# A hybrid decoder layer: the token-major copies of k and v are made by VectorE and DRAM instead of TensorE

## The chip, the cores and the metric

The kernel runs on one core of one Trainium2 chip. The metric is device time in microseconds (us) of one launch. Before the change it is 2226.82 us, the median of three runs (2225.97 to 2227.2).

## The reference, cut to what matters

One layer works on 16 meta tokens followed by 2048 tokens of width 1024. After an RMS norm one projection makes everything: for the gated DeltaNet 8 heads of q, k, v and a gate z (128 columns each), for the short convolution four more groups of 1024 columns. For a head the recurrence is

```python
S = S * gl + einsum('cd,ce->de', k_dec, v_new)      # once per chunk
v_new = u - einsum('cd,de->ce', w, S)
o = einsum('cd,de->ce', q_dec, S) + einsum('ij,je->ie', qk, v_new)
```

The projection produces k and v with the 128 channels on the partitions and the tokens along the free axis (channel-major). The recurrence needs k (scaled by a decay, `kd`) and v (scaled by the inverse norm of k, `vr`) with the tokens of a chunk of 128 on the partitions (token-major). The change is about how these two copies are made. The output is the layer's result with the residual added, after a last RMS norm.

## The kernel before, in words

The tokens are worked on in two halves of 1024 (`hf` 0 and 1). Each half has 8 slots, one per head; head number `i` runs from 0 to 15 over both halves. A slot is a list of projection jobs (`slot_jobs`, L825): q, k, c, h, b, the short convolution's gate, v, z. A job (`run_group`, L750) multiplies 128 columns of the input projection with all tokens of the half in three passes of split float32 (`wh*hh`, `wh*hl`, `wl*hh`), for which one 512 KB block of weights `wr` is loaded (`load_w`), rounded by ScalarE into `wh`, and subtracted by VectorE into `wl`. Both the raw block and the split are double buffered.

TensorE's instructions are put in order by hand: generators (streams) yield the time they want to wait by a planner's model of every engine (`Model`, L30), and `pump` (L234) resumes those that are due between the matmuls of the jobs. The order of TensorE, VectorE, ScalarE and GpSimd is the program order that comes out of this. The order of the DMA issues on SyncE's queue is not fixed by hand; each issue waits there for its semaphores, in order.

For each head these streams run beside the jobs of later slots:

- `delta_front` (L975): the decay matrix E, the products k·k and q·k, and a substitution of 32 steps on VectorE (`nb`, `XT`), which needs k and q of the head. Its result goes to DRAM (`xtd`).
- `normalize` (L526, first half only): the norm of a block of tokens of the second half. It uses the buffers tagged `kd`, `gw` and `Q`.
- `delta_back` (L1124): loads the blocks of the inverse (`W<-xtd`, L1135), loads `qd` (L1140), turns k, v and q with TensorE (L1148 to L1177), and merges the 32-blocks of the inverse to 128-blocks in four steps of small matmuls (`X`, `Q`, `W`, `p1` to `p4`).
- `delta_scan` (L1304): the recurrence over 8 chunks, with `kd`, `vr`, `qd`, `W`.
- `delta_out` (L1354): norm, gate and store.

`held` and `hold` (L581) keep two streams from using one buffer tag at a time: `ta` for the two PSUM banks of the streams, `Q` and `gw` for two SBUF buffers. In `delta_back` each of the six groups of four transposes (two each for k, v and q) goes through a `ta` bank: ScalarE reads k's with the scale `cd`, VectorE reads v's with the scale `ir`, ScalarE squares q's. The done mark `("vr", i)` lets the v job of the next slot overwrite `vT` (`pre_v`, L841).

After the two halves comes the output projection: 32 units of 48 matmuls (`unit_mm`, L1459).

Of the kernel before, what the change touches and what calls it, by code (L numbers as in the profile page):

```python
# [9 lines left out]
F32 = mybir.dt.float32  # L10
# [9 lines left out]
NM = 16  # L20
NH = 8
# [152 lines left out]
def hybrid_trunk(  # L174
# [23 lines left out]
    xtd = tc.dram_tile([2, 32, 32, 32], F32, name="xtd")  # L198
    ged = tc.dram_tile([2, NH * 9, 128], F32, name="ged")
    nmd = tc.dram_tile([2, NM, NM], F32, name="nmd")  # L200
    gtd = tc.dram_tile([2, NH * 9, 128], F32, name="gtd")
# [29 lines left out]
    def start(gen):  # L231
        streams.append([gen, clk()])
# [350 lines left out]
    def hold(tag="ta", keep=False):  # L583

        while tag in held:
            yield 0.2
        if keep:
            held.add(tag)

    G = {}  # L590
# [384 lines left out]
    def delta_front():  # L975

        for i in range(2 * NH):
# [144 lines left out]
            done.add(("front", i))  # L1122

    def delta_back():  # L1124

        for i in range(2 * NH):
# [18 lines left out]
            vr = vt(dp, [128, NC, 128], "vr")  # L1145
            while ("conv", hf, 16 + hd, LAST[hf]) not in done:
                yield 0.3
            for b4 in range(2):  # L1148
                cs = slice(4 * b4, 4 * b4 + 4)
                yield after(slot=(pta, "ta"), least=0.3)  # L1150
                yield from hold()
                pk = ptile(pta, "ta", [128, 4, 128])
                for c in range(4):
                    tr(pk[:, c, :], k_[:, 4 * b4 + c, :])
                for c in range(4):
                    cc = 4 * b4 + c
                    nc.scalar.activation(kd[:, cc], pk[:, c, :], AF.Copy, scale=cd[:, cc : cc + 1])
                yield after(d["vT"], slot=(pta, "ta"), least=0.3)
                yield from hold()
                pv = ptile(pta, "ta", [128, 4, 128])  # L1160
                for c in range(4):
                    c0 = m0 + 128 * (4 * b4 + c)
                    tr(pv[:, c, :], d["vT"][:, c0 : c0 + 128])
                nc.vector.tensor_tensor(
                    out=vr[:, cs],
                    in0=pv,
                    in1=ir[:, cs].unsqueeze(2).to_broadcast([128, 4, 128]),
                    op=ALU.mult,
                )
                yield after(slot=(pta, "ta"), least=0.3)  # L1170
                yield from hold()
                pq = ptile(pta, "ta", [128, 4, 128])
                for c in range(4):
                    tr(pq[:, c, :], q_[:, 4 * b4 + c, :])
                for c in range(4):
                    cc = 4 * b4 + c
                    nc.scalar.activation(junk[:, 0:128], pq[:, c, :], AF.Square, accum_out=ssq[:, cc : cc + 1])  # L1177
            done.add(("vr", i))
            egl = vt(dp, [128, NC], "egl")

            yield after(W)
            for a in (0, 64, 32):
# [14 lines left out]
            for a in (0, 64):  # L1197
                nc.scalar.activation(Q[a + 32 : a + 64, :, 0:32], p1[a + 32 : a + 64, :, 0:32], AF.Copy)
            nc.vector.tensor_copy(egl, qd[:, :, 127])
            nc.vector.tensor_tensor(out=qd, in0=qd, in1=q_, op=ALU.mult)  # L1200
# [27 lines left out]
            nc.scalar.mul(W[0:64, :, 64:128], p4[0:64], -1.0)  # L1228
            yield after(W, qd)
            blocks[i] = dict(egl=egl, kd=kd, vr=vr, P=P, qd=qd, cj=B["cj"])  # L1230
# [163 lines left out]

    LANDING = 3.0
    STEP = 1.0
    SUBST = 0.8
# [108 lines left out]
    pump()  # L1506
    start(delta_front())
    start(delta_back())
    start(delta_scan())
# [142 lines left out]
```

## Time and profile before

| | us |
|---|---|
| median of three runs | 2226.82 |
| profiled execution, its own time | 2231.35 |
| its span in the trace | 2229.6 |
| TensorE (PE) busy | 2176.5 |
| VectorE (DVE) busy | 1454.9 |
| ScalarE (ACT) busy | 851.3 |
| GpSimd (POOL) busy | 195.8 |

Busy time is the time in which at least one instruction of the engine was running; PE is the matrix multiply, PEld its weight load. "L118" stands on nearly all rows, since a helper records every instruction; so the rows are told apart by the names of their tiles: `ta<-ident,k` is a transpose of k into a `ta` bank. The share of the DMA engines is the mean over the core's 16.

### The profile page before, as it was taken

The numbers are of one execution on the slowest core, as the hardware profiler recorded it, in microseconds if no ns is written. First come the engines' busy times: TensorE is split into PE (matmuls) and PEld (weight loads), VectorE is DVE, ScalarE is ACT, GpSimd is POOL, SyncE is SP. The second block draws the span as 40 slices with busy tenths as digits, with TensorE's granted clock in tenths as the row PEclk, the third lists the DMA queues.
The fourth block names the chain that finished last, engine by engine and source line by source line (L and its number), as shares of the span: only waits on it lengthen the run. The fifth ranks groups of instructions, "written<-read, shape, count | busy, mean of one in ns | idle before, by whom it ended". The sixth has DMA issues, their size and how long they took to land.

```text
span 2229.6 us, 35449 instructions
## 1 busy us (share of the span) xinstructions
PE 2176.5 (98%) x13472; PEld 1917.2 (86%) x13472; DVE 1454.9 (65%) x3911; ACT 851.3 (38%) x1991; POOL 195.8 (9%) x361
## 2 busy tenths in 40 slices
PE   6999999999999999999999999999999999999998
PEld 5999999999999999878888888888878887788886
DVE  4677777777777777776767767676657683444222
ACT  5533434343434444443434352434342533322111
POOL 4010101010101010201010110010000100000000
PEclk9999999999999999999999999999989998999999
DMA  5434444353548844534254424353846443645321
GB/s 141 82 79 67 84 72 94 64 97 60 100 56 108 88 88 62 131 54 77 55 78 54 82 51 87 50 83 65 66 37 73 88 118 114 212 157 188 114 90 57
DMA packets 257096, 196.26 MB, mean 88 GB/s; under 512 B 61957, under 2 KB 226318, under 8 KB 256926
## 3 DMA queue, kind: packets, MB, share of 16 engines
q1 hardware_dynamic: 256926, 194.00, 46.0%
q8 instruction: 106, 1.74, 0.3%
q14 instruction: 64, 0.52, 0.1%
HBM read 157.89 MB, written 36.06 MB: 87 GB/s over the span
## 4 chain that ended last, share of the span: by engine, by line
PE 92%; DMA 2%; DVE 2%; ACT 2%; issue 1%; SPq 0%; POOLq 0%; ACTq 0%; DVEq 0%
PE mm L118 78%; PE ta L118 7%; PE rec L118 4%; PE o L118 3%; DMA wr<-in_w_in_dram 1%; ACT junk L118 1%; SPq L118 0%; DVE prod L118 0%; DVE hl L118 0%; DMA xtd<-XT 0%; DMA wr<-mixd 0%; DMA ysd<-raw 0%; DVE XT L118 0%; DVE acc L118 0%; ACT hh L118 0%
## 5 line engine op out<-in xcount | busy, mean ns | idle before, releaser
L118 PE MATMUL mm<-hh,wh 128*128 128x512 f32 (+3 forms) x2816 | 1006.3, 365 | 10.2 <-ACT hh L118 8.6
L118 PE MATMUL mm<-hl,wh 128*128 128x512 f32 (+3 forms) x2816 | 986.2, 358 | 0.2 <-DVE hl L118 0.2
L118 PE MATMUL mm<-hh,wl 128*128 128x512 f32 (+3 forms) x2816 | 641.4, 360 | 4.6 <-DVE wl L118 4.6
L118 PEld LDWEIGHTS mm<-hh,wh 128*128 128x128 f32 x2816 | 532.0, 190 | 61.5 <-ACT hh L118 9.8
L118 PEld LDWEIGHTS mm<-hl,wh 128*128 128x128 f32 x2816 | 531.9, 189 | 47.5 <-DVE hl L118 1.1
L118 PEld LDWEIGHTS mm<-hh,wl 128*128 128x128 f32 x2816 | 480.7, 189 | 53.6 <-DVE wl L118 5.5
L118 DVE TENSOR_TENSOR wl<-wr,wh 128x512 fp32r<-128x512 f32 x348 | 230.5, 685 | 69.3 <-ACT wh L118 34.1
L118 DVE SCALAR_TENSOR_TENSOR acc<-raw,pcol,acc 128x384 f32<-128x384 f32 (+2 forms) x360 | 231.3, 644 | 50.3 <-ACT acc L118 42.5
L118 ACT ACTIVATE wh<-wr 128x1024 fp32r<-128x1024 f32 x178 | 187.9, 1056 | 133.8 <-PE mm L118 88.1
L118 DVE SCALAR_TENSOR_TENSOR prod<-nb,XT 128x8 f32<-128x8 f32 (+30 forms) x496 | 194.3, 392 | 11.2 <-DMA nb<-nbd 6.4
L118 DVE TENSOR_REDUCE XT<-prod 128x8 f32<-128x16 f32 (+30 forms) x496 | 147.3, 297 | 17.1
L118 ACT ACTIVATE raw<-mm 128x384 f32<-128x384 f32 (+2 forms) x120 | 61.7, 514 | 227.8 <-PE mm L118 227.7
L118 ACT ACTIVATE vn<-rec,cj 128x128 f32<-128x128 f32 x128 | 46.9, 367 | 219.2 <-PE rec L118 218.8
L118 ACT ACTIVATE sc_c<-mm 128x384 f32<-128x384 f32 (+3 forms) x82 | 42.3, 516 | 176.1 <-PE mm L118 169.7
L118 PE MATMUL mm<-oh,wh 128*128 128x512 f32 x256 | 101.9, 398 | 0.0
L118 PE MATMUL mm<-ol,wh 128*128 128x512 f32 x256 | 100.4, 392 | 0.0
L118 DVE SCALAR_TENSOR_TENSOR yy<-rec,neg,vr 128x128 f32<-128x128 f32 x128 | 44.6, 349 | 71.6 <-PE rec L118 70.8
L118 DVE TENSOR_TENSOR y<-mm,y 128x512 f32<-128x512 f32 x23 | 15.9, 692 | 111.4 <-PE mm L118 111.4
L118 ACT ACTIVATE ojk<-y 128x512 bf16<-128x512 f32 x23 | 14.5, 631 | 183.4 <-DVE y L118 127.2
L118 POOL TENSOR_TENSOR opy<-mo,nhalf 128x4 f32<-128x4 f32 x32 | 33.7, 1052 | 509.4 <-DVE mo L118 509.4
L118 ACT ACTIVATE acc<-mm,pcol 128x384 f32<-128x384 f32 (+2 forms) x120 | 72.1, 601 | 0.1
L118 DVE SCALAR_TENSOR_TENSOR S<-S,egl,rec 128x128 f32<-128x128 f32 x104 | 35.8, 344 | 53.8 <-PE rec L118 53.5
(242 smaller groups left out, 2530.3 us busy)
## 6 DMA issues: line engine op xcount, KB each, us to landing
wr<-in_w_in_dram SPq DMA_DIRECT2D x128, 512.0 KB, 7.9
wr<-mixd SPq DMA_DIRECT2D x50, 512.0 KB, 4.5
E<-gtd SPq DMA_DIRECT2D x16, 512.0 KB, 3.8
qd<-ged SPq DMA_DIRECT2D x16, 512.0 KB, 3.9
nb<-nbd SPq DMA_DIRECT2D x64, 128.0 KB, 4.4
mixd<-zs SPq DMA_DIRECT2D x32, 256.0 KB, 2.4
out_dram<-y SPq DMA_DIRECT2D x16, 512.0 KB, 2.6
kd<-in_x_dram SPq DMA_DIRECT2D x9, 512.0 KB, 9.8
```

The source lines that it names most:

```text
L118: r = real(*args, **kw)
```

## The change

A new stream `delta_turn` runs for each head. Once all of k (and later all of v) of the head has been made, it takes each in two halves of four chunks. VectorE transposes the 32 x 32 blocks of a [128, 512] piece into a buffer (`gw` and `Q` in turn), and four DMAs of 64 KB write the buffer to a DRAM tile `kvd`, each block to its transposed place, in runs of 32 floats. `delta_back` waits for the mark `("turned", i)`, keeps only the two groups of transposes of q, and loads `kd` and `vr` token-major from `kvd` behind the load of `W`. GpSimd multiplies `kd` by its scale in the middle of the merges, VectorE multiplies `vr` at their end.

```diff
+    kvd = tc.dram_tile([2, 2, NC, 128, 128], F32, name="kvd")
...
+    def turn_out(dram, src, tmp):
+        nc.vector.transpose(out=tmp.rearrange("p c i -> p (c i)"), in_=src.rearrange("p c i -> p (c i)"))
+        for a in range(4):
+            nc.sync.dma_start(
+                dram[:, :, 32 * a : 32 * a + 32].rearrange("c (b y) x -> y (c b) x", b=4),
+                tmp[32 * a : 32 * a + 32].rearrange("y c (b x) -> y (c b) x", b=4),
+            )
...
+    def delta_turn():
+        for i in range(2 * NH):
+            hf, hd = divmod(i, NH)
+            m0 = NM if hf == 0 else 0
+            while i >= 2 and ("blocks", i - 2) not in done:
+                yield 0.3
+            for w in range(2):
+                while ("conv", hf, (8, 16)[w] + hd, LAST[hf]) not in done:
+                    yield 0.3
+                src = slot[i]["k"] if w == 0 else slot[i]["vT"][:, m0 : m0 + HALF].rearrange("p (c i) -> p c i", i=128)
+                for c2, tag in enumerate(("gw", "Q")):
+                    yield after(src, slot=(dp, tag), eng="DVE", lag=0.3)
+                    yield from hold(tag, True)
+                    cs = slice(4 * c2, 4 * c2 + 4)
+                    turn_out(kvd[i % 2, w, cs], src[:, cs], vt(dp, [128, 4, 128], tag))
+                    if w and c2:
+                        done.add(("vr", i))
+                    yield DRAIN
+                    held.discard(tag)
+            done.add(("turned", i))
...
     def delta_back():
...
-            while ("conv", hf, 16 + hd, LAST[hf]) not in done:
+            while ("turned", i) not in done:
                 yield 0.3
             for b4 in range(2):
-                cs = slice(4 * b4, 4 * b4 + 4)
-                yield after(slot=(pta, "ta"), least=0.3)
-                yield from hold()
-                pk = ptile(pta, "ta", [128, 4, 128])
-                for c in range(4):
-                    tr(pk[:, c, :], k_[:, 4 * b4 + c, :])
-                for c in range(4):
-                    cc = 4 * b4 + c
-                    nc.scalar.activation(kd[:, cc], pk[:, c, :], AF.Copy, scale=cd[:, cc : cc + 1])
-                yield after(d["vT"], slot=(pta, "ta"), least=0.3)
-                yield from hold()
-                pv = ptile(pta, "ta", [128, 4, 128])
-                for c in range(4):
-                    c0 = m0 + 128 * (4 * b4 + c)
-                    tr(pv[:, c, :], d["vT"][:, c0 : c0 + 128])
-                nc.vector.tensor_tensor(
-                    out=vr[:, cs],
-                    in0=pv,
-                    in1=ir[:, cs].unsqueeze(2).to_broadcast([128, 4, 128]),
-                    op=ALU.mult,
-                )
                 yield after(slot=(pta, "ta"), least=0.3)
                 yield from hold()
                 pq = ptile(pta, "ta", [128, 4, 128])
...
-            done.add(("vr", i))
             egl = vt(dp, [128, NC], "egl")
-            yield after(W)
+            yield after(W) + 1.5
+            for w, t_ in enumerate((kd, vr)):
+                nc.sync.dma_start(t_, kvd[i % 2, w].rearrange("c t j -> t c j"))
...
+            nc.gpsimd.tensor_tensor(
+                out=kd, in0=kd, in1=cd.unsqueeze(2).to_broadcast([128, NC, 128]), op=ALU.mult
+            )
             nc.vector.tensor_copy(egl, qd[:, :, 127])
...
             nc.scalar.mul(W[0:64, :, 64:128], p4[0:64], -1.0)
-            yield after(W, qd)
+            yield after(vr, eng="DVE", lag=0.3) + 1.0
+            nc.vector.tensor_tensor(
+                out=vr, in0=vr, in1=ir.unsqueeze(2).to_broadcast([128, NC, 128]), op=ALU.mult
+            )
+            yield after(W, qd, kd, vr)
...
+    DRAIN = 4.0
...
+    start(delta_turn())
```

## Rows read from the trace of the kernel before

**Rows 1.** The page: busy us of two engines; the chain that ended last.

```profile
PE 2176.5 (98%) x13472; PEld 1917.2 (86%) x13472; DVE 1454.9 (65%) x3911; ACT 851.3 (38%) x1991; POOL 195.8 (9%) x361
PE 92%; DMA 2%; DVE 2%; ACT 2%; issue 1%; SPq 0%; POOLq 0%; ACTq 0%; DVEq 0%
```

**Rows 2.** Windows: stretch, length, PE, PEld, DVE, ACT, POOL busy, clock, DMA share, GB/s.

```profile
64.00:1830.00 1766.00, 1750.05 (x11457) 1569.94 (x11457) 1281.78 (x3579) 723.99 (x1759) 159.84 (x271) 1.00 0.47 76
700.00:745.00 45.00, 45.00 (x289) 44.97 (x288) 38.24 (x115) 16.67 (x37) 4.42 (x10) 1.00 0.97 113
1625.00:1638.00 13.00, 13.00 (x101) 10.34 (x101) 5.30 (x10) 3.37 (x6) 0.49 (x1) 0.50 0.52 65
```

**Rows 3.** Groups by shape, TensorE: busy us, mean ns | idle before, releaser.

```profile
L118 PE MATMUL ta<-ident,vT 128*128 128x128 f32 x128 | 20.0, 279 | 1.3 <-ACT junk L118 0.7
L118 PE MATMUL ta<-ident,k 128*128 128x128 f32 x128 | 19.2, 272 | 0.7 <-DVE vr L118 0.7
```

**Rows 4.** Timeline of TensorE, head 4: start us, duration us, instruction.

```profile
633.95 0.34 PE L118 MATMUL mm<-hl,wh 128*128 128x384 f32 x1
634.12 0.60 PE L118 MATMUL ta<-ident,k 128*128 128x128 f32 x4
634.48 0.42 PE L118 MATMUL mm<-hh,wh 128*128 128x384 f32 x1
634.74 0.34 PE L118 MATMUL mm<-hl,wh 128*128 128x384 f32 x1
```

**Rows 5.** Groups by shape, VectorE.

```profile
L118 DVE TENSOR_TENSOR vr<-ta,ir 128x512 f32<-128x512 f32 x32 | 22.1, 691 | 28.1 <-PE ta L118 27.9
L118 DVE STREAM_TRANSPOSE X<-W 32x256 f32<-32x256 f32 x48 | 20.7, 432 | 11.8 <-DMA W<-xtd 10.8
L118 DVE TENSOR_TENSOR E<-E,cj 128x1024 f32<-128x1024 f32 x16 | 19.8, 1235 | 0.0
```

**Rows 6.** Queue in 636 to 641 us (W loads alone): packets, MB, share of 16 engines.

```profile
q1 hardware_dynamic: 1100, 0.13, 17.1%
```

**Rows 7.** The same in 673 to 676.4 us, mostly the four nbd writes.

```profile
q1 hardware_dynamic: 1251, 0.21, 34.8%
```

**Rows 8.** DMA issues of the whole run: count, KB each, median us to landing.

```profile
wr<-in_w_in_dram SPq DMA_DIRECT2D x128, 512.0 KB, 7.9
sc_c<-xnd SPq DMA_DIRECT2D x3, 512.0 KB, 3.6
```

**Rows 9.** Timeline of SyncE's queue, head 4: its qd load, then its xtd stores.

```profile
579.65 0.34 SPq L118 DMA_DIRECT2D qd<-ged  x1
629.85 2.13 SPq L118 DMA_DIRECT2D xtd<-XT  x4
```

**Rows 10.** Timeline: v of heads 4 and 11 complete (ScalarE), head 11's transposes (TensorE).

```profile
582.84 0.51 ACT L118 ACTIVATE vT<-acc 128x384 f32<-128x384 f32 x1
1377.17 0.63 ACT L118 ACTIVATE vT<-acc 128x512 f32<-128x512 f32 x1 [1.56 <-DVE acc L118]
1389.11 0.60 PE L118 MATMUL ta<-ident,k 128*128 128x128 f32 x4
```

**Rows 11.** Timeline: a weight rounded after a late load; idle us and releaser in brackets.

```profile
737.07 1.06 ACT L118 ACTIVATE wh<-wr 128x1024 fp32r<-128x1024 f32 x1 [0.86 <-DMA wr<-in_w_in_dram]
```

**Rows 12.** Timeline near 932 us: GpSimd, VectorE twice, TensorE.

```profile
931.73 2.81 POOL L118 TENSOR_TENSOR wl<-wr,wh 128x1024 fp32r<-128x1024 f32 x1 [1.59 <-ACT wh L118]
931.47 0.14 DVE L118 SCALAR_TENSOR_TENSOR msm<-mnb,mXT 16x5 f32<-16x5 f32 x1
932.56 2.00 DVE L118 SCALAR_TENSOR_TENSOR msm<-mnb,mXT 16x6 f32<-16x6 f32 x1
935.23 0.66 PE L118 MATMUL ta<-ident,sc_c 128*128 128x128 f32 x4 [1.85 <-DVE hl L118]
```

**Rows 13.** Timeline near 1620 us, head 13's merge: VectorE, TensorE.

```profile
1619.63 0.43 DVE L118 STREAM_TRANSPOSE X<-W 32x256 f32<-32x256 f32 x1 [7.20 <-DMA W<-xtd]
1620.16 0.22 PE L118 MATMUL ta<-X,E 32*32 32x32 f32 x2 [1.57 <-ACT junk L118]
```

## The prediction

> **What bounds the kernel now.** I read the engine table and the chain first [rows 1]: TensorE is busy for 2176.5 us of a span of 2229.6, and 92% of the chain that ended last is its own work. VectorE has 65%. The windows say the same of the stage that the change touches [rows 2]: from 64 to 1830 us, where the heads are worked on, TensorE is busy for 1750.05 of 1766 us and VectorE for 1281.78 (73%). So in this stage an edit is worth what it takes out of TensorE's stream, less what it makes TensorE wait. The DMA engines are at 0.47 there, but not evenly: from 700 to 745 us they are at 0.97 with only 113 GB/s [rows 2], and there one weight block was rounded 0.86 us late for its load [rows 11]. So that is the place where more DMA work has no cover. A stop can cost more than its length: at head 13 VectorE waited 7.20 us for W's blocks, TensorE stood for 1.57 us before its merge matmuls [rows 13], and from 1625 to 1638 us the granted clock was 0.50, the 1.2 GHz level [rows 2]; 13 us at half speed lose about 6.5.
>
> **What is removed.** 128 transposes of k and 128 of v [rows 3], in 64 groups of four. The busy sums of 20.0 and 19.2 us overlap with their neighbours, so I take a group from the timeline [rows 4]. It starts at 634.12, and the next matmul starts 0.36 us later; the one after that comes after 0.26 where the pitch was 0.17, so 0.09 more is lost. That is 0.45 a group, 28.8 us for 64. The idle time ahead of these transposes goes too, 1.3 and 0.7 us [rows 3]. Together 30.8 us. Bounds: 23.0 (0.36 a group) and 41.2 (39.2 busy and 2.0). ScalarE loses 128 scaled copies; it is busy for 38% [rows 1] and sets nothing, so I count nothing for it.
>
> **What VectorE takes on.** 64 block transposes of 128 x 512. The nearest row is a block transpose of 32 x 256 in 0.432 us; a product over 512 elements takes 0.691 [rows 5], so I take 0.70, that is 44.8 us. Bounds: 0.432 (if the size were free) and 0.864 (twice the row), 28 to 55 us. The scaling of v becomes 16 products of 128 x 1024 between SBUF operands, as `E<-E,cj` at 1.235 [rows 5], 19.8 us, for 32 at 0.691 that go, 22.1 us. Net 42.5 us, so VectorE goes from 73% to 75% of the stage. Its idle quarter hides that. Without the cover it costs at most 42.5 us; I put 1 us for late moments. The transposes must be done before `("vr", i)`, but that mark now comes before the merges instead of in `delta_back`, so the next v job cannot wait longer for it.
>
> A rule speaks against this exchange. The Trainium skill ("VectorE: DVE Perf Modes", section "Rules for kernel authors") gives 128 x 128 transposes to TensorE where a PSUM destination will do, since VectorE turns blocks of 32 only. By it the 0.11 us a transpose would be well spent and nothing would be won. By the rows the engine that gives up the time is the bound and the one that takes it on is not, and the sum is minus 30.8 us.
>
> **What the DMA queue takes on.** Each head adds 16 stores of 64 KB in runs of 128 bytes (512 packets each, 8192 a head, 131072 in all) and two loads of 512 KB in runs of 512 bytes (32 loads, 1024 packets each). Two rows price packets of 128 bytes: the loads of W, 1100 packets in 5 us at 17.1% of 16 engines [rows 6], are 12.4 ns of one engine each; a stretch of 3.4 us with `nbd` stores, 1251 packets at 34.8% [rows 7], gives 15.1. The other end is a packet of a weight load: 7.9 us [rows 8] for 64 packets on each engine, 123 ns. The stores here have the run length of the first two, so I take 15.1: 124 us of all 16 engines over the kernel, 7.7 a head (102 to 1008 at the ends). A load lands in 3.6 us from a contiguous block and in 7.9 from strided weights [rows 8]; `kvd` is contiguous but read in short runs, so I take 5: 160 us, 10 a head (115 to 253). So the DMA engines go from 0.47 to about 0.63 of the stage. Over most of it nothing waits for them. From 700 to 745 us, with 0.97 in use, the v stores of head 5 and its two loads, up to 14 us of work, come on top of weight loads that were already late [rows 11]. Lower bound 0, upper 14; I take 6 us, once.
>
> On SyncE's queue 288 issues are added, at 0.34 us for a single one to 0.53 in a group of four [rows 9], 98 to 153 us spread over the run. A store waits there for its block transpose and a load for the stores' landing, and what is queued behind them is the next weight load. Its waiters are ScalarE's `wh` and then TensorE. The text of the change puts the loads behind W's blocks, but the queue does not keep the program's order: head 4's `qd` load, which the program has behind `front`, went out at 579.65, 50 us ahead of that head's `xtd` stores [rows 9]. I expect the same of `kd` and `vr`: issued when the stores have landed and the tiles are free, in the first half well ahead of W.
>
> **What moves.** `delta_back` now waits for the turn, two pieces of v at no less than 0.70 plus DRAIN's 4.0 us by the planner, 9.4 us after v is there. In the first half v is complete 51 us before (582.84 against transposes at 634.12 [rows 4, 10]). For head 11 it was 12 us (1377.17 against 1389.11 [rows 10]), so in the second half some merges start later by a few us. Behind them waits only the recurrence; TensorE has jobs to run meanwhile, and I count nothing.
>
> **GpSimd's product** is new in the middle of the merges, 16 of 128 x 1024. The nearest row is the same shape of `wl`: 2.81 us [rows 12]. It is hidden on GpSimd, at 9% [rows 1], but not from VectorE: while that product ran, a VectorE instruction of 0.14 us took 2.00, and TensorE then stood for 1.85 us on VectorE's `hl` [rows 12]. Bounds on TensorE: 0 and 16 x 1.85 = 29.6 us. In the first half `kd` should be there early, so that GpSimd runs the product while VectorE waits for W's blocks (10.8 us of idle before its X transposes in the run [rows 5]). In the second half `kd` lands during the merges of a few heads. I take 5 us.
>
> **The sum.** Minus 30.8 (transposes), plus 1 (VectorE), 6 (weight loads), 5 (GpSimd): about minus 19. On the profiled execution's own 2231.35 us that is 2212; the median of the runs shown is 4.5 us (0.2%) lower than it, so I forecast 2208 us. About 0.2%, some 4.5 us, is also what a measurement of this kernel can tell from no change.
>
> **Rivals.**
>
> A. TensorE pays for GpSimd's product in every head. For it: the 1.85 us above. Against: VectorE idles in this place, and TensorE has matmuls that need nothing of VectorE. At 1.85 a head 29.6 us are given back, and two stops that drop the clock as at 1625 us cost 13 more: 2227 - 31 + 30 + 13 = 2239 us, slower. It decides from 1.9 us a head on, where the gain is gone. The Trainium skill has this as a rule ("SBUF — State Buffer", section "Who interferes with whom"): a VectorE instruction with two SBUF inputs and a GpSimd instruction that reads SBUF block each other for the whole instruction; rows 12 agree, 2.00 us for 0.14. Chance 0.13.
>
> B. The DMA engines become the bound in their slow stretches, and weight loads arrive late. For it: 0.97 in use and a late load [rows 2, 11]. Against: the average is 0.47. If four heads lose 10 us each and two clock drops follow, 2227 - 31 + 40 + 13 = 2249 us. It decides from 31 us of late loads. Chance 0.10.
>
> C. The gain is mostly eaten by small waits: a stream that holds `Q` and `gw` delays the merges and `normalize`, and stores in front of weight loads cost 1 to 2 us in each head, 24 us: 2220 us. For it: one queue serves all DMAs. Against: the idle time of TensorE in the stage is 16 us in 1766, so the cover has held so far. Chance 0.09.
>
> **How the numbers follow.** Forecast 0.68 (about 2196 to 2219, faster), A 0.13, B 0.10, C 0.09. C gives faster in two thirds of its cases, else same; A gives same in a third of its cases, slower in the rest; B slower, save a fifth that is same. That is faster 0.74, same 0.09, slower 0.17. The range goes from 2193 (no cost, and a gain of 34) to 2238 (most of A).
>
> **What would show it.** Right: TensorE has 256 transposes fewer and about 29 to 39 us less busy time in the stage; block transposes of 128 x 512 near 0.70 us; `kvd` stores near 15 ns a packet, the DMA share near 0.63; `kd` loads issued before W's in the first half; VectorE instructions of 2 us beside `kd` on GpSimd. The forecast is wrong if TensorE's idle time in the stage grows from 16 us by more than 20, and the releaser tells which rival it is: VectorE or merges for A, `wh` behind a `wr` load between 700 and 745 us for B. If the transposes are gone and the span shrinks by less than 10 us with no new waits, my price of 0.45 us a group was wrong.

## The result and the profile after

The changed kernel takes 2255.51 us (median of 4 runs, 2250.66 to 2260.2) against 2227.01 (2225.97 to 2227.65) beside it: a ratio of 1.0118, 95% interval 1.0095 to 1.0141. The forecast was 2208, the range 2193 to 2238. It is slower, by about 26 us. Where a ratio is turned into microseconds below, it is taken times 2227.

The page of the profiled run (2258.27 us, span 2256.6): busy time of the engines, then the chain that ended last.

```profile
PE 2165.1 (96%) x13216; PEld 1912.0 (85%) x13216; DVE 1492.7 (66%) x3967; ACT 821.8 (36%) x1867; POOL 230.1 (10%) x377
PE 84%; DMA 7%; DVE 5%; SPq 2%; ACT 1%; issue 1%; POOLq 0%; ACTq 0%; DVEq 0%
```

Against [rows 1] the span is 27.0 us longer while TensorE is busy for 11.4 us less: its idle time went from 53.1 to 91.5 us. TensorE's share of the chain fell from 92 to 84%, and what came in is DMA (2 to 7%), VectorE (2 to 5%) and SyncE's queue (0 to 2%). VectorE is still far from full.

The windows of the changed kernel (columns as in [rows 2]):

```profile
64.00:1845.00 1781.00, 1725.08 (x11118) 1552.96 (x11117) 1289.45 (x3573) 682.52 (x1612) 191.49 (x285) 0.98 0.59 93
700.00:745.00 45.00, 39.22 (x248) 38.65 (x248) 28.11 (x106) 14.21 (x40) 2.74 (x5) 0.96 0.85 117
690.00:800.00 110.00, 90.33 (x560) 87.93 (x558) 63.90 (x195) 36.68 (x98) 10.69 (x22) 0.92 0.91 97
792.00:808.00 16.00, 6.22 (x97) 5.76 (x98) 5.46 (x12) 1.13 (x3) 2.02 (x2) 0.57 0.55 68
```

In the stage TensorE now idles for some 56 us where it idled for 16 [rows 2]. From 690 to 800 us it is busy for 90.33 of 110 us; the same window of the kernel before had 109.83, with the DMA engines at 0.76 in place of 0.91. From 792 to 808 us the granted clock is 0.57, mostly the 1.2 GHz level, after a stop of TensorE. Summed over the whole run from 60 us on in slices of 5 us, (1 - granted clock) times length is 23 us before and 48 after: a measure of what the slower clock costs.

The groups by shape:

```profile
L118 POOL TENSOR_TENSOR kd<-kd,cd 128x1024 f32<-128x1024 f32 x16 | 31.7, 1979 | 18.3 <-issue 18.3
L118 DVE STREAM_TRANSPOSE X<-W 32x256 f32<-32x256 f32 x48 | 20.8, 432 | 40.2 <-DMA W<-xtd 39.3
L118 DVE TENSOR_TENSOR vr<-vr,ir 128x1024 f32<-128x1024 f32 x16 | 19.5, 1217 | 0.0
L118 DVE STREAM_TRANSPOSE Q<-k 128x512 f32<-128x512 f32 x16 | 11.3, 704 | 0.8 <-PE ta L118 0.8
```

A block transpose of 128 x 512 takes 0.704 us, the product of v 1.217, GpSimd's product 1.98. The row that moved is `X<-W`: VectorE's idle time ahead of it for W's blocks is 39.3 us, against 10.8 [rows 5]. TensorE's idle time ahead of the first matmuls of the merges, which read `X`, grew with it, first before, then after:

```profile
L118 PE MATMUL ta<-X,E 32*32 32x32 f32 x512 | 11.7, 195 | 2.3 <-ACT junk L118 1.6 <-DVE X L118 0.7
L118 PE MATMUL ta<-X,E 32*32 32x32 f32 x512 | 13.8, 202 | 29.6 <-DVE X L118 17.6 <-issue 11.9
```

That is 27.3 of the 38.4 us that TensorE idles more. The part named "issue" has no releaser in the trace; its longest piece, 8.20 us, stands at head 13 where VectorE also waits for W.

The DMA queue and issues (KB each, median us to landing):

```profile
q1 hardware_dynamic: 426814, 230.71, 56.2%
wr<-in_w_in_dram SPq DMA_DIRECT2D x128, 512.0 KB, 9.0
kvd<-gw SPq DMA_DIRECT2D x128, 64.0 KB, 5.9
kvd<-Q SPq DMA_DIRECT2D x128, 64.0 KB, 2.5
vr<-kvd SPq DMA_DIRECT2D x16, 512.0 KB, 8.6
```

A weight load lands in 9.0 us for 7.9 [rows 8].

**Head 5, the largest single stop.** The last reduction that completes `XT` runs on VectorE from 770.69 us. SyncE's queue, in order:

```profile
770.15 0.34 SPq L118 DMA_DIRECT2D xnd<-kd  x1
771.76 6.66 SPq L118 DMA_DIRECT2D kvd<-gw  x4
778.46 5.61 SPq L118 DMA_DIRECT2D kvd<-Q  x4
784.18 0.44 SPq L118 DMA_DIRECT2D wr<-in_w_in_dram  x1
784.67 5.28 SPq L118 DMA_DIRECT2D xtd<-XT  x4
789.99 0.45 SPq L118 DMA_DIRECT2D kd<-kvd  x1
798.85 1.78 SPq L118 DMA_DIRECT2D W<-xtd  x4
```

Eight stores of the next head's k go out between the end of `XT` and its own stores, and the first four of them occupy the queue for 6.66 us; the four `xtd` stores behind them take 5.28, where head 4's took 2.13 [rows 9]. `xtd` goes out 13.6 us after `XT` is there, and W's loads follow 8.9 us behind its last store. VectorE and TensorE at that place:

```profile
770.69 0.42 DVE L118 TENSOR_REDUCE XT<-prod 128x8 f32<-128x256 f32 x1
800.65 0.43 DVE L118 STREAM_TRANSPOSE X<-W 32x256 f32<-32x256 f32 x1 [15.44 <-DMA W<-xtd]
801.23 0.28 PE L118 MATMUL ta<-X,E 32*32 32x32 f32 x2 [12.95 <-DVE X L118]
```

Thirty us pass from `XT` to the `X` transposes (12.9 in the kernel before), VectorE stands for 15.44 us, TensorE for 12.95. Head 13 repeats it: eight stores from 1635.15, `xtd` at 1649.65, W's loads at 1665.49, VectorE's wait 10.14 us.

### The profile page after: what moved, and what is told of

It is laid out like the page before. It is cut to its first block, busy times and chain, and to the rows that moved or that the text cites. A ratio compares the mean times of both kernels' runs of the same rounds, so it can differ in the third digit from the quotient of the medians.

```text
span 2256.6 us, 35369 instructions
## 1 busy us (share of the span) xinstructions
PE 2165.1 (96%) x13216; PEld 1912.0 (85%) x13216; DVE 1492.7 (66%) x3967; ACT 821.8 (36%) x1867; POOL 230.1 (10%) x377
## 3 DMA queue, kind: packets, MB, share of 16 engines
q1 hardware_dynamic: 426814, 230.71, 56.2%
## 4 chain that ended last, share of the span: by engine, by line
PE 84%; DMA 7%; DVE 5%; SPq 2%; ACT 1%; issue 1%; POOLq 0%; ACTq 0%; DVEq 0%
PE mm L118 72%; PE ta L118 6%; PE rec L118 4%; PE o L118 2%; SPq L118 2%; DMA xtd<-XT 2%; DMA W<-xtd 1%; DMA wr<-in_w_in_dram 1%; DVE prod L118 1%; DMA gw<-in_norm_g_dram 1%; DMA nb<-nbd 1%; DMA kd<-in_x_dram 1%; DMA sc_c<-xnd 1%; DVE XT L118 1%; DVE sc_y L118 1%
## 5 line engine op out<-in xcount | busy, mean ns | idle before, releaser
L118 PEld LDWEIGHTS mm<-hh,wh 128*128 128x128 f32 x2816 | 535.9, 191 | 65.2 <-ACT hh L118 11.8
L118 DVE TENSOR_TENSOR wl<-wr,wh 128x512 fp32r<-128x512 f32 x356 | 237.7, 689 | 74.7 <-ACT wh L118 54.5
L118 DVE SCALAR_TENSOR_TENSOR yy<-rec,neg,vr 128x128 f32<-128x128 f32 x128 | 44.5, 348 | 65.2 <-PE rec L118 64.8
L118 DVE TENSOR_TENSOR y<-mm,y 128x512 f32<-128x512 f32 x21 | 14.5, 691 | 101.1 <-PE mm L118 101.1
L118 POOL TENSOR_TENSOR kpy<-ssk,nhalf 128x8 f32<-128x8 f32 x16 | 27.6, 1723 | 485.5 <-DVE ssk L118 437.8
```

The costliest lines, as they stand in the source:

```text
L118: r = real(*args, **kw)
```

## The experiments

Eighteen kernels ran. The theories that their expectations name: Q, the stores' and loads' place ahead of `xtd` and W on SyncE's queue; P, in `b_no_turn`, that the transposes' price was wrong; P, from `a_wide` on, that the stores' packets of 128 bytes fill the DMA engines (PQ is that together with Q); G, GpSimd's product holds VectorE (rival A of the prediction); D, the amount of work on the 16 DMA engines, whatever its order; theories B and E, that this price falls in the stretches that were full before, or on every head alike.

**1. Taking the change apart.** Four kernels: `b_no_turn` is the kernel before without the k and v transposes, `a_no_dma` the changed kernel without stores and loads, the other two have the one or the other.

```diff
# b_no_turn (of the kernel before; the same for v)
-  tr(pk[:, c, :], k_[:, 4 * b4 + c, :])
-  nc.scalar.activation(kd[:, cc], pk[:, c, :], AF.Copy, scale=cd[:, cc : cc + 1])
+  nc.scalar.activation(kd[:, cc], k_[:, cc, :], AF.Copy, scale=cd[:, cc : cc + 1])
# a_no_dma (a_stores_only keeps the first, a_loads_only has loads of the same shape from x)
-  for a in range(4): nc.sync.dma_start(dram[...], tmp[...])
-  nc.sync.dma_start(t_, kvd[i % 2, w].rearrange("c t j -> t c j"))
-  in0=kd / in0=vr
+  in0=k_
```

> The kernel before without the 64 groups of transposes of k and v and without anything in their place: kd and vr are scaled copies of the channel-major k, so the output is not the layer's. Theory Q (the transposes were worth what was forecast, and the changed kernel loses more than that because its own DMAs stand in front of the xtd stores and the W loads): 2227 - 31 = 2196 us, 2190 to 2202. Rival P (a group of transposes was worth less than 0.45 us, the time was hidden elsewhere): 2212 us or more.

> The changed kernel without the stores to kvd and without the loads from it: VectorE's block transposes, GpSimd's product and VectorE's product stay, the products read the channel-major k, so the output is not the layer's. Theory Q: VectorE waits no longer than before for W's blocks (10.8 us in the run, where the changed kernel has 39.3), TensorE keeps its 2.4 GHz clock, 2195 to 2208 us. Rival G (GpSimd's product stops VectorE, or VectorE has too much to do): nothing of this is taken away, so 2235 us or more.

> The changed kernel with the stores to kvd and without the loads from it: the products read the channel-major k, so the output is not the layer's. Theory Q with the stores as the larger part (the next head's 16 stores are issued in front of the xtd stores): 2225 to 2250 us. Theory Q with the loads as the larger part (1 MB between the xtd stores and the W loads): 2200 to 2215 us. Rival G: as the changed kernel, 2245 us or more, with VectorE's idle time before X as before the change.

> The changed kernel without the stores to kvd, the loads of kd and vr taken from the input x with the same runs of 512 bytes, so the output is not the layer's. They have no store to wait for, so they may go out earlier than in the changed kernel. Theory Q with the stores as the larger part: 2200 to 2215 us. Theory Q with the loads as the larger part: 2225 to 2250 us. Rival G: 2245 us or more.

| kernel | us | ratio (95%) |
|---|---|---|
| b_no_turn | 2214.35 | 0.9936 (0.9919 to 0.9952) |
| a_no_dma | 2223.75 | 0.9971 (0.9956 to 0.9986) |
| a_stores_only | 2250.18 | 1.0108 (1.0089 to 1.0127) |
| a_loads_only | 2221.9 | 0.997 (0.9954 to 0.9985) |

The engine row of `b_no_turn`:

```profile
PE 2148.4 (97%) x13216; PEld 1897.0 (86%) x13216; DVE 1455.3 (66%) x3915; ACT 854.5 (39%) x1993; POOL 202.6 (9%) x361
```

TensorE is busy for 28.1 us less than in [rows 1], so the price of a group (28.8 for 64) was right as busy time. The time falls by 14 us alone, to 2214.35: theory Q's 2190 to 2202 is missed, and the figure lies where theory P put it, at 2212 or more. P's reason holds in so far as the transposes' time had been hiding something else; the price of the busy time was not wrong. TensorE's idle time grows from 53.1 to 67.3 us, and 9.8 of these 14.2 us stand ahead of the merges, with no store of k or v in the way:

```profile
L118 PE MATMUL ta<-X,E 32*32 32x32 f32 x512 | 12.7, 201 | 12.1 <-ACT junk L118 6.5 <-issue 4.2 <-DVE X L118 1.4
```

VectorE's wait for W doubles (21.7 us in 7 places). In the kernel before, head 5's six groups of transposes run from 752.24 to 758.23 us, across W's loads, which are issued at 754.64, and the merge starts at 759.90 without a stop. So a likely reason, which no run tests alone, is that the transposes were also the work that filled the wait for W.

The stores carry nearly all of the loss: 0.0137 of ratio, 30.5 us, over `a_no_dma`. The loads alone cost nothing (0.997 against 0.9971). `a_no_dma` lies between the ranges of Q and G, and `a_loads_only` 7 us above Q's, as fits when half of the transposes' gain is missing. `a_stores_only` reaches the upper end of Q's range and is within G's too; VectorE's wait for W, 34.2 us, speaks for Q. The queue's rows with and without the stores, first of `a_no_dma`, then of `a_stores_only`:

```profile
q1 hardware_dynamic: 257646, 195.57, 47.7%
```

```profile
q1 hardware_dynamic: 393534, 213.94, 53.4%
```

Times the spans (2224.1 and 2246.1) that is 1061 and 1199 us of all 16 engines: 138 us for the stores, 16.9 ns for each of their 131072 packets (16.3 if it is spread over the 135888 by which the rows differ), where the prediction had taken 15.1. So their size was known; what waits for it was not.

**2. Place in the queue, or the engines?**

```diff
# a_k_late
+  while i and ("wl", i - 1) not in done: yield 0.3      # in delta_turn, ahead of k
   yield after(W) + 1.5
+  done.add(("wl", i))
# a_own_queue
-  nc.sync.dma_start(dram[...], tmp[...])
+  nc.gpsimd.dma_start(dram[...], tmp[...])
# fix1: a_k_late; in the second half v waits for ("wl", i) too; loads issued behind W's;
#       the wait for "turned" and GpSimd's product moved behind the merges
# a_kd_act
-  nc.gpsimd.tensor_tensor(out=kd, in0=kd, in1=cd..., op=ALU.mult)
+  nc.scalar.activation(kd[:, c], kd[:, c], AF.Copy, scale=cd[:, c : c + 1])   # 8 a head, behind the last merge
```

> The changed kernel, but a head's k is turned and stored only once the W blocks of the head before it have landed; v as before. Theory Q (the stores stand on SyncE's queue and on the DMA engines ahead of the xtd stores and the W loads, so VectorE and then TensorE wait for W): most of the waits for W went behind k's stores, so 2228 to 2242 us, with VectorE's waits for W ahead of the X transposes under 25 us in place of 39 in the profiled run, and the clock loss under 35 us in place of 47. Rival D (it is the amount of DMA work, wherever it stands in the order): 2250 to 2262 us. Rival G (GpSimd's product): 2250 to 2262 us.

> The changed kernel with the kvd stores alone issued from GpSimd's queue in place of SyncE's; same packets, same loads. Theory Q in its narrow form (the one in-order queue of SyncE is what holds xtd and W): 2226 to 2240 us, and the W loads go out within 7 us of the last row of XT at head 5. Rival D (the 16 DMA engines are full with 128-byte packets and the queue does not matter): 2248 to 2262 us. In between, 2240 to 2248, both have a part. GpSimd's selects that make E may come later behind a waiting store, which would add some us in either case.

> The changed kernel with the scaling of kd by cd moved from GpSimd to ScalarE (8 scaled copies a head, behind the last merge). Theory Q: GpSimd's product mostly ran while VectorE waited for W anyhow, so 2248 to 2258 us, at most 7 us under the changed kernel. Rival G (GpSimd's product holds VectorE in the merges, 1 to 2 us a head): 2225 to 2240 us.

> The changed kernel with k's stores behind the W loads of the head before, in the second half v's stores behind the head's own W loads, the kd and vr loads queued behind W's loads, and delta_back waiting for the turn only after the merges, where GpSimd's product then runs. Theory Q: no kvd store or load stands ahead of xtd and W, so the waits for W return to those of the kernel without the k and v transposes: 2212 to 2228 us. Rival D (amount of DMA work): 2245 to 2260 us. If the recurrence then waits for vr and kd instead, 2228 to 2245 us, with TensorE's waits at vn and hh.

| kernel | us | ratio (95%) |
|---|---|---|
| a_k_late | 2241.38 | 1.0056 (1.0038 to 1.0074) |
| a_own_queue | 2257.42 | 1.0147 (1.013 to 1.0164) |
| a_kd_act | 2289.48 | 1.0282 (1.0265 to 1.0299) |
| fix1 | 2242.74 | 1.008 (1.0061 to 1.0099) |

The order is worth 14 us: `a_k_late` lies in Q's range and not in D's or G's, and of Q's two signs VectorE's waits for W came under 25 us (23.5), while the clock loss stayed above 35 (37). The move to GpSimd's queue brings no time. SyncE's queue and then VectorE at head 5 of `a_own_queue`, and what SyncE's queue waited for between 763.5 and 776 us:

```profile
757.61 5.03 SPq L118 DMA_DIRECT2D xtd<-XT  x3
762.73 0.40 SPq L118 DMA_DIRECT2D xnd<-kd  x1
763.17 0.54 SPq L118 DMA_DIRECT2D xtd<-XT  x1
772.73 0.38 SPq L118 DMA_DIRECT2D kd<-kvd  x1
773.28 1.44 SPq L118 DMA_DIRECT2D W<-xtd  x3
...
777.51 1.36 DVE L118 STREAM_TRANSPOSE X<-W 32x256 f32<-32x256 f32 x3 [9.60 <-DMA W<-xtd]
...
SPq L118 <- DMA xnd<-kd: 9.0, 1, 9.0
```

No store of k stands ahead of `xtd` any more, and it still takes 10 us from its last issue to W's loads. But at this place that is the queue's order again: the head's own `kd` load stands ahead of W's, and by the profile the queue waits there for 9.0 us until `normalize`'s store `xnd<-kd` has read the tile, with the DMA engines at 0.70 (763.7 to 772.7 us). Head 13 shows the other case; GpSimd's stores are issued at 1626.94 and from 1632.62 to 1635.25, and SyncE's queue has:

```profile
1633.32 2.18 SPq L118 DMA_DIRECT2D xtd<-XT  x2
1636.30 7.83 SPq L118 DMA_DIRECT2D xtd<-XT  x2
1653.62 1.78 SPq L118 DMA_DIRECT2D W<-xtd  x4
```

Here two `xtd` stores take 7.83 us to issue with no store of k or v on their queue, while the DMA engines are full (1.16 from 1633 to 1644.2 us; this share can read above 1), and W's loads then wait 9.3 us for `xtd`. The Trainium skill ("DMA: Bandwidth & Descriptors", section "Issuing engines are not separate DMA queues") says that transfers started by another engine run interleaved on the same 16 DMA engines, and only the issuing time is saved. Head 13 agrees.

Theory Q in its narrow form missed both of its signs (2226 to 2240 us; W's loads within 7 us of `XT`, measured 15.7). The test is not a clean one, though. VectorE's waits for W fell to 17.7 us from 39.3, but the 256 issues occupy GpSimd for 168 us, and with long runs (`a_wide_own` below) the same move costs 18 us. So what the queue alone is worth stays open.

`a_kd_act` fell outside every expectation, 36 us slower than the changed kernel: ScalarE's 128 copies (390 ns each) stand behind the last merge, and a wait of TensorE for ScalarE's `Q` (11.0 us) comes up, and VectorE's for its `X` grows to 31.2 us from 15.4. It says nothing of GpSimd; that ScalarE has 62% idle does not make it free at that place. `fix1` brought VectorE's waits for W down to 7.7 us in its trace and TensorE's idle time ahead of the merges to 6.1, and still took 2242.74. GpSimd then waits for `kd`'s load, 112.5 us in 11 places, and TensorE idles for 79.7 us in all; which of its other waits sets the time, no run shows. Short waits for W are not enough.

**3. The length of the runs, and GpSimd.**

```diff
# a_wide: the same stores and bytes, in runs of 2 KB (a_wide_56: heads 5 and 6 alone)
-  dram[:, :, 32 * a : 32 * a + 32].rearrange("c (b y) x -> y (c b) x", b=4),
-  tmp[32 * a : 32 * a + 32].rearrange("y c (b x) -> y (c b) x", b=4),
+  dram.rearrange("c t j -> (c t j)")[q : q + 128 * 128].rearrange("(y f) -> y f", y=32),   # q = 128 * 128 * a
+  tmp[32 * a : 32 * a + 32].rearrange("y c x -> y (c x)"),
# a_no_dma_kd: a_no_dma, and
-  nc.gpsimd.tensor_tensor(out=kd, in0=k_, in1=cd..., op=ALU.mult)
# gather: stores as in a_wide; behind W's loads, kd and vr each in 8 loads of 64 KB
+  nc.sync.dma_start(t_[32 * b : 32 * b + 32, 4 * u : 4 * u + 4].rearrange("y c (a x) -> y c a x", a=4),
+      g_d.rearrange("(a y c z) -> y c a z", a=4, y=32, c=4)[:, :, :, 32 * b : 32 * b + 32])
```

> The changed kernel with the kvd stores in runs of 2 KB in place of 128 bytes (each store writes its 32 partitions to a contiguous stretch, so the tokens of kd and vr come out in the wrong places): same number of stores, same bytes, same places in the queues, same waits. Theory P (the packets of 128 bytes fill the 16 DMA engines in the stretches that were full before, and everything else that passes through them, xtd and W above all, comes late): 2222 to 2236 us, DMA packets down by about 123000, VectorE's waits for W under 20 us in place of 39. Rival Q (what costs is the place of the stores in SyncE's queue, whatever their runs): 2246 to 2258 us.

> As the kernel with wide runs, but for heads 5 and 6 alone, whose stores fall on 640 to 860 us. If the loss of the stores sits mostly in the stretch from 700 to 800 us, where the DMA engines were full already (X transposes 14 us late at head 4 and 42 late at head 5 against the kernel before): 2232 to 2244 us. If each head pays about the same, a gain of 2 parts in 16 of some 26 us, 3 us: 2249 to 2257 us.

> The kernel with VectorE's block transposes but without kvd's stores and loads, and now also without the scaling of kd on GpSimd (the recurrence takes k itself). Rival G (GpSimd's product holds VectorE in the merges): the 8 us between the kernel without the transposes (ratio 0.9936) and the one without stores and loads (0.9971) come back, 2211 to 2217 us. If they belong to VectorE's block transposes and the changed order of the work: 2219 to 2226 us.

> The changed kernel with the short runs on the other side: the stores write 2 KB runs, and kd and vr are loaded in 16 loads of 64 KB in runs of 128 bytes, queued behind W's loads. The same result as the kernel before. Theory P with the order (short packets cost where they stand ahead of xtd and W): 2224 to 2242 us. If only the number of short packets counts, wherever they stand: 2246 to 2262 us.

| kernel | us | ratio (95%) |
|---|---|---|
| a_wide | 2238.84 | 1.004 (1.0028 to 1.0052) |
| a_wide_56 | 2248.51 | 1.0084 (1.0058 to 1.011) |
| a_no_dma_kd | 2213.84 | 0.9928 (0.9906 to 0.995) |
| gather | 2273.12 | 1.0196 (1.0169 to 1.0223) |

Long runs give back 17 us, not all 30: P's range (2222 to 2236) and Q's (2246 to 2258) are both missed. One reason is in the queue's row: 303934 packets, 122880 fewer, and still 53.7% of the span, 1204 us, 86 more than with the loads alone (50.4% of 2218.5). The bytes are still there. The other, as I read it then, was the order. SyncE's queue at head 5 of `a_wide`, and VectorE:

```profile
759.15 4.07 SPq L118 DMA_DIRECT2D kvd<-gw  x4
763.27 6.25 SPq L118 DMA_DIRECT2D kvd<-Q  x4
769.56 2.50 SPq L118 DMA_DIRECT2D xtd<-XT  x4
...
785.89 1.37 DVE L118 STREAM_TRANSPOSE X<-W 32x256 f32<-32x256 f32 x3 [13.41 <-DMA W<-xtd]
```

Four stores of 2 KB runs hold the queue for 6.25 us too, while the DMA engines are at 0.95. So the length of the runs alone does not make an issue slow.

`a_wide_56`, long runs in heads 5 and 6 alone, gives back 0.0034, 7.6 us, where an even share of the 17 would be 2. Its interval overlaps that of the changed kernel (1.0095 to 1.0141), so it decides little.

`gather` came out above both of its ranges: with the short runs behind W's loads the time rises by 17 us over the changed kernel. Its chain, and one head's loads on SyncE's queue:

```profile
PE 75%; DMA 10%; SPq 7%; DVE 5%; ACT 2%; issue 1%; POOL 0%; DVEq 0%; POOLq 0%; ACTq 0%
```

```profile
656.23 9.71 SPq L118 DMA_DIRECT2D kd<-kvd  x7
665.98 5.92 SPq L118 DMA_DIRECT2D vr<-kvd  x8
```

Fifteen loads occupy the queue for 15.6 us, and VectorE then waits for `vr` (31.2 us in all).

`a_no_dma_kd` answers for GpSimd and VectorE at once: without stores, loads and GpSimd's product the kernel is at 0.9928, that of `b_no_turn` within the intervals. VectorE's 64 block transposes, with all else in which the two kernels differ, thus cost nothing that can be measured. Taking the product out is worth 0.0043, 9.6 us, in that kernel; the two intervals (0.9956 to 0.9986 and 0.9906 to 0.995) nearly touch. That VectorE's blocking is the reason is not shown. TensorE idles as long with the product as without (65.3 and 65.2 us), and what differs is the loss to the slower clock (35 and 25 us). The longest stop of `a_no_dma`, 8.88 us at 1017.90, stands where VectorE's block transpose waits 16.49 us for a store to free `gw`. The blocking itself shows in the changed kernel; GpSimd and VectorE at head 6:

```profile
911.09 1.89 POOL L118 TENSOR_TENSOR kd<-kd,cd 128x1024 f32<-128x1024 f32 x1
...
911.08 2.18 DVE L118 TENSOR_TENSOR sc_y<-sc_y,sc_c 128x256 f32<-128x256 f32 x1 [1.39 <-ACT sc_c L118]
```

A product of 128 x 256 on VectorE took 2.18 us, where the other seven of its kind take about 0.42. That is the rule of the Trainium skill that the prediction cites ("SBUF — State Buffer", section "Who interferes with whom"), and the trace agrees in some six of 16 heads. It goes both ways: at head 7 VectorE's `qd`, started during GpSimd's select for `E`, took 2.12 us where it took 1.23 at head 5, and GpSimd's product, started at 1051.31 while `qd` ran, took 2.86 in place of 1.89.

**4. Are these all?**

```diff
# a_wide_late: a_wide and a_k_late.  a_wide_own: a_wide and a_own_queue.
# a_no_kd: the changed kernel without GpSimd's product.  a_wide_late_no_kd: all three prices taken away.
```

> Wide runs for kvd's stores (2 KB) and k's stores only behind the W loads of the head before, together. Theory PQ (half of the stores' price is their short packets, the other half their place ahead of xtd on SyncE's queue, as at head 5 of the kernel with wide runs, where 8 stores took the queue from 759.15 to 769.52 us and xtd went out behind them): a further gain over wide runs alone, 2221 to 2232 us. If the rest of the price has another cause (the tiles that the stream holds, the wait of the merges for the turn): 2235 to 2243 us.

> Wide runs for kvd's stores, issued from GpSimd's queue in place of SyncE's. Theory PQ: xtd no longer stands behind the stores, 2222 to 2233 us, unless GpSimd's other work comes late behind a store that waits, which was seen in the kernel with short runs on that queue (398 us of GpSimd's time behind `kvd` stores). If the place in SyncE's queue does not matter: 2235 to 2245 us.

> The changed kernel without the scaling of kd on GpSimd (the recurrence takes the unscaled kd), all else as it is. If GpSimd's product has a price of its own that adds to the others (2223.75 against 2213.84 us in the kernels without stores and loads): 2243 to 2249 us. If in the changed kernel it hides in the waits for W: 2252 to 2258 us.

> Wide runs, k's stores behind the W loads of the head before, and no scaling of kd on GpSimd: all three suspected prices taken away, while VectorE's block transposes, the stores, the loads and the wait of the merges for the turn stay. If these three are the whole cause: 2211 to 2222 us, near the kernel without the transposes (2214.35). If something of the change is still unpriced: 2226 us or more.

| kernel | us | ratio (95%) |
|---|---|---|
| a_wide_late | 2238.17 | 1.0049 (1.0034 to 1.0064) |
| a_wide_own | 2256.09 | 1.0122 (1.0105 to 1.0139) |
| a_no_kd | 2255.73 | 1.0127 (1.0109 to 1.0145) |
| a_wide_late_no_kd | 2234.34 | 1.0022 (1.0007 to 1.0037) |

My next theory, short runs plus place in the queue, fell as well. Each alone gives back 14 to 17 us and both together 15, so they do not add. The likely reading is that they remove in part the same waits: TensorE's idle time ahead of the merges is 29.6 us in the changed kernel, 20.6 in `a_k_late`, 22.5 in `a_wide` and 16.8 with both. `a_wide_own` is above both of its ranges, 18 us slower than `a_wide`. Taking GpSimd's product out, worth 9.6 us where no store is in the way, is worth nothing in the changed kernel (`a_no_kd`); that VectorE waits for W there anyhow is the likely reason, and not a tested one. With everything taken away that I had named, 21 us are still lost against `a_no_dma_kd`. SyncE's queue of `a_wide_late_no_kd` shows where some of it may sit:

```profile
700.84 6.24 SPq L118 DMA_DIRECT2D kvd<-gw  x4
...
708.14 6.84 SPq L118 DMA_DIRECT2D kvd<-Q  x4
...
720.43 3.94 SPq L118 DMA_DIRECT2D vr<-kvd  x1
724.42 4.14 SPq L118 DMA_DIRECT2D mixd<-zs  x1
...
759.96 1.82 SPq L118 DMA_DIRECT2D xtd<-XT  x4
...
763.69 7.79 SPq L118 DMA_DIRECT2D W<-xtd  x4
```

These are v's stores and load, in long runs, from 700 to 725 us, in the stretch that was at 0.97 before [rows 2]; even W's four loads take 7.79 us to issue.

**5. By place.** The stores and loads of heads 5, 6, 13 and 14 alone are left out, or alone kept.

```diff
-  for a in range(4):
+  for a in range(4 if go else 0):     # go: i not in (5, 6, 13, 14), or i in (5, 6, 13, 14); the loads alike
```

> The changed kernel without kvd's stores and loads in four of the 16 heads (5, 6, 13 and 14: there kd and vr are made from k), whose stores fall on 635 to 860 and 1600 to 1780 us, the two stretches in which the DMA engines were full or nearly so in the kernel before (shares 0.77 to 0.96 from 660 to 780 us, 0.80 from 1580 to 1620, 0.75 from 1700 to 1740); the other 12 heads keep theirs. Theory B (the price of the DMA work falls where the engines are full already, and there in all its forms: short packets, bytes, held issues): most of the 28 to 31 us comes back, 2226 to 2238 us. Rival E (every head pays its share): a quarter, 2246 to 2252 us.

> The counterpart: kvd's stores and loads in those four heads alone, none in the other 12. Theory B: most of the price stays, 2240 to 2252 us. Rival E: a quarter of it on top of the kernel without stores and loads (2223.75), 2229 to 2234 us.

`a_skip4` took 2237.75 us, 1.0036 (1.0014 to 1.0057); `a_only4` 2231.09, 1.0005 (0.9992 to 1.0017). Leaving out four heads of 16 gives back 18 us, as theory B says (2226 to 2238). But the four alone add only 7.6 us to `a_no_dma`, a quarter of the whole, as theory E says. Neither holds: 18 us the one way, 7.6 the other. The twelve other heads alone cost 14.5; 7.6 and 14.5 make 22 of 32.7. By the medians the price of a head's DMA work is higher in those four heads (1.9 us each against 1.2 alone), and 10.7 us arise only when all heads have it. That the lateness of the others is the reason is a reading, not shown.

The start of the first `X` transpose, from the timelines, shows the course (us):

| head | before | changed | a_no_dma_kd | a_wide_late_no_kd | a_only4 |
|---|---|---|---|---|---|
| 0 | 206.9 | 214.4 | 214.9 | 213.2 | 213.2 |
| 4 | 642.3 | 656.4 | 644.7 | 643.8 | 649.6 |
| 5 | 758.3 | 800.6 | 764.4 | 778.4 | 772.8 |
| 10 | 1293.5 | 1360.5 | 1337.0 | 1333.2 | 1325.8 |
| 13 | 1619.6 | 1667.3 | 1635.1 | 1639.8 | 1632.5 |
| 15 | 1838.3 | 1893.6 | 1848.8 | 1863.6 | 1858.8 |

From head 4 to head 5 the changed kernel falls back by 28 us, the one without DMA work by 4, those between by 19 and 7. In the middle every version is 32 to 67 us late, also the one that ends 15 us earlier than the kernel before, so the lateness of one head cannot be read as lost time.

None of the versions that compute the whole beats the kernel before: the best of them is `a_k_late`, at 1.0056.

## Why the prediction was wrong

**The step that failed is "What the DMA queue takes on".** Its sizes held: 16.9 ns a packet for 15.1, a DMA share in the stage of 0.59 for 0.63, `kd` and `vr` loads ahead of W as expected (of head 5, `vr` at 735.88, but `kd` only at 789.99, between `xtd` and W), and the loads cheaper than thought (57 us of all 16 engines between `a_no_dma` and `a_loads_only`, for 160). What failed is the sentence "Over most of it nothing waits for them", with 6 us, once, at the weight loads, and "what is queued behind them is the next weight load". Queued behind them are also the four `xtd` stores, and behind those W's four loads, a chain of two small transfers for which VectorE stands at its `X` transposes and TensorE behind it. The row was there: head 13's wait of 7.20 us for W [rows 13] was read as an example of what a stop costs, and not as the place where the next one would be. The term measured 30.5 us for the stores, in place of 6; the 2.2 for the loads on top of them cannot be told from zero. TensorE's idle time ahead of the merges is 12.3 us in `a_no_dma` and 29.6 in the changed kernel, 17.3 of the 26.2 us by which all its idle time differs.

**The mechanism is rival B's, with another victim.** B made the weights late; TensorE waits 5.5 us for `wl` (4.6 before), and the chain has 1% for weight loads, as before, against the 29.6 us ahead of the merges. B's price, 40 us and two clock drops, was near: 38.4 us more of idle time, and half-clock stretches behind the stops. TensorE is busy for 16.7 us more than in `b_no_turn` for the same 13216 matmuls, and the loss to the clock, summed as above, is 48 us against 23 there; so the slower clock took back more than half of the 28.1. That B came near in size is partly luck, since its stops were to be at the weights. Its chance, 0.10, was too low: 0.97 of the DMA engines over 45 us was read as one place, and its weight was taken from the mean of 0.47.

**"What is removed" was right as busy time and wrong as time.** 28.8 priced, 28.1 measured, but only 14.3 us of time in `b_no_turn`. The sum set what leaves TensorE's stream equal to time, on the ground that the stage had 16 us of idle time. Of those 28 us 14 turned into new idle time, 9.8 of it ahead of the merges (2.3 to 12.1 us). Even with no DMA price the time would have been about 2213 (0.9936 of 2227), within the range but 5 above the forecast.

**"What VectorE takes on" was right in its prices**: 0.704 us for 0.70, 1.217 for 1.235, and nothing lost on the whole (0.9928 against 0.9936); the 1 us set for it cannot be told from zero. It left out that a block transpose can wait for its buffer, 16.49 us once in `a_no_dma`. The Trainium skill ("VectorE: DVE Perf Modes", section "Rules for kernel authors") would have kept these transposes on TensorE. Its advice came out right here, though not by VectorE's time: what cost was the way through DRAM that the blocks of 32 make needed.

**"GpSimd's product"**: 5 us taken, 9.6 measured where no store or load is in the way, none in the changed kernel. Rival A's mechanism is in the trace; what it costs by itself no run shows.

**"What moves"** counted nothing for the merges' wait. No run took that wait alone away; `fix1`, which moved it behind the merges together with other things, was not faster than `a_k_late`.

**Still open**: whether half of the transposes' 28 us turned into waits because they had filled the wait for W, what SyncE's queue alone is worth, and how the 30 us of the stores divide between short packets, bytes and order. The three overlap, and 21 us remain with the first and third removed.

## What to carry to other kernels

Before transfers are added, list for each stretch in which the DMA engines are near full every small transfer that an engine stands and waits for, and put the price there, not at the mean share; here GpSimd's queue did not help, and a later place did in part. A busy time taken off the bound engine need not come back as time: in this kernel, at 98% busy, half of it came, so ask what wait the removed work had filled. And prices measured one at a time do not add: taking out the same product was worth 9.6 us in one version and nothing in the next.

## What the runs showed of the hardware

- Four stores of 64 KB took 1.95 us of SyncE's queue at 635.01 us, with the DMA engines at 0.45, and 6.66 at 771.76, with the engines at 1.01; in long runs too (6.84 at 708.14 in `a_wide_late_no_kd`, at 1.01). Of the four at 771.76 one alone took 0.56 us and the last 2.98; of W's four loads at 763.69 in that kernel 0.42 and 4.02, at 1.02. Full engines do not always slow an issue: in the kernel before, four `xtd` stores took 2.04 us at 745.83 with the engines at 1.03.
- Runs of 2 KB in place of 128 bytes cut the packets of the stores to a sixteenth, but their time on the engines only from some 150 us (56.2% of 2256.6 less the 1118 with the loads alone) to 86.
- GpSimd's queue moves the same stores in 8192 packets (3.4% of the span, 77 us), at 0.65 to 0.67 us of GpSimd for each of the 256 issues, without any gain in time.
